# A hybrid RWKV-7 and band-attention block on one core: longer pauses between the steps of the recurrence's solve and chain, split head sums, and two tiles moved to other slots

## The chip, the core and the metric

The kernel runs on one core of a Trainium2 chip. The metric is the device time of one execution in microseconds. The time before is 867.89 us, the median of 3 runs (867.29 to 868.58). One execution was also recorded by the hardware profiler; all durations below are from it.

## What is computed

One residual block over 256 tokens of width 2048, in float32. The input is normalised and multiplied by one wide matrix, whose columns feed two branches; the branches are gated, projected, merged and sent through an output matrix. Cut to what matters:

```python
h = _rms_norm(x, pre_norm_g[l])
proj = h @ w_in[l]
p_r, p_k, p_v, z_r, q_a, k_a_att, v_a, z_a, m_r, m_a = jnp.split(proj, split_points, axis=-1)
y_r = _rwkv7_mixer(h, p_r, p_k, p_v, ...) * jax.nn.silu(z_r)
y_a = _chunk_band_attention(q_a, k_a_att, v_a, rel_bias[l]) * jax.nn.silu(z_a)
merged = (jax.nn.sigmoid(m_r + b_merge[l, 0]) * (y_r @ w_branch_rwkv[l])
          + jax.nn.sigmoid(m_a + b_merge[l, 1]) * (y_a @ w_branch_attn[l]))
x = x + _rms_norm(merged @ w_out[l], post_norm_g[l])
```

The RWKV-7 mixer is a recurrence over tokens for each of 16 heads of 64 channels, with a 64 by 64 state per head:

```python
sa = jnp.einsum('bhvk,bhk->bhv', state, -kkt)
state = (state * wt[:, :, None, :] + sa[..., None] * (kkt * at)[:, :, None, :]
         + vt[..., :, None] * kt[..., None, :])
yt = jnp.einsum('bhvk,bhk->bhv', state, rt)
```

## The kernel before

**The large products.** The weights arrive in chunks of 512 KB on SP's queue (three raw buffers, `NR`). ACT rounds a chunk to its high part (`wh_...`, line 92), DVE subtracts to get the low part (`wl_...`, line 93); there are four buffers of each (`NH`, `NL`), so that the low part of a chunk waits for the products of the chunk four before it. PE multiplies each high part with both halves of the activation (128x512) and each low part with the high half (128x256, lines 346 and 348). A product of 256 columns is four chunks long: `r`, `k` and `v` for the recurrence, `zr` and `za` for the gates, `q` and `ak` for attention. `va` and the later ones are 512 columns wide, and eight chunks long. A number behind a name is its first head pair: q2 covers the tiles 2 and 3; a digit behind that is the chunk (`wl_ak23` is the last chunk of ak2).

**Accumulators.** The large products share two accumulators in PSUM (`pm`, tag "mm", `acc_...`). `take` (lines 387 to 393) empties one: ACT copies one half, then DVE adds the other. The product after the next starts when that is done. All small products share four smaller ones (`ps`).

**The recurrence** is done in chunks of 64 tokens, for two groups of 8 heads (4 tiles, or two "duos" of two tiles). `group_decay` and `duo_front` (one for the duos 0, 2, 4, 6) build each duo's factors: head sums by a product with ones (`pn`, `pb`, through `head_sums`), decays (`pc`), the rate (`pa`), a long run on DVE, then the products of v (`pv`) and the chunk matrices A (`pA`). `group_back` then does for the whole group: the inverse of 16 by 16 blocks on DVE (`pr` and `S`, lines 599 and 601), from and to DRAM (`nb`, `N`, `rb`, `RA`, issued on ACT's queue); the solve (`T`, `z` line 620, `xx` line 628, `T2`, `z2` line 637, `x2` line 646, the transposes `pt` line 657 and their copies `BT`); and the chain over the four chunks c: `pw` (lines 667 and 671), its copy W on ACT (673), `pu` (677), its copies UV on DVE and ACT (679, 680), `pg` (691) and `py` (686, 694), and the new state SB on DVE (702, 704). pg and pw of the next chunk wait for UV and SB. In the trace a group's digit is left out of names; in the order it stands first (pg10 is group 1, chunk 0).

**What sets the order.** `run_plan` issues the large products chunk by chunk and prepares chunks two ahead. After each chunk `pump` takes steps of the small work, which is written as Python generators: up to `quota` steps of the queue `side` (the fronts), then `BQ` = 2 steps of the queue `back` (group_back, gates, attention). A step goes from one `yield` to the next. The plan after the projections of the recurrence is `q0 r2 v0 z0 v1 r6 r0 z2 q2 q4 q6 z4 r4 z6`, where q stands for q and ak, r for zr, z for za and v for va. A scheduler with a timeline of its own then orders each engine's instructions by the program's order and its own estimate, so that a step can move by some products.

**Slots that tie things.** The tile for q4 and later, `late`, takes the slot "A" (line 932) of group 1's A, and is free only when the chain of group 1 is done. The gate of za2 lies in a slot of tag "BT" (line 922), and its take waits for pg10 in both kernels; until then acc_za2 holds one of the two accumulators.

Of the kernel before, what the change touches and what calls it, by code (L numbers as in the profile page):

```python
# [9 lines left out]
F32 = mybir.dt.float32  # L10
# [9 lines left out]
QF = 2  # L20
QB = 2
BQ = 2
# [15 lines left out]
P = 128  # L38
D = 2048
DB = 1024  # L40
# [21 lines left out]
def kernel(ctx: ExitStack, tc, x, xt, vecs, w_in, wa1, w2, a2, w0, rel, w_br, w_ba, w_out, post_g, bm, out):  # L62
# [5 lines left out]
    bg = ctx.enter_context(tc.tile_pool(name="bg", bufs=1))  # L68
    tp = ctx.enter_context(tc.tile_pool(name="tp", bufs=2))
# [4 lines left out]
    def small(name):  # L74
        return ps.tile([P, 512], F32, tag="sm", name=name)
# [15 lines left out]
    def split(h, l, src, go=False):  # L91
        queue(ACT.activation(h, src, AF.Copy), go)  # L92
        queue(DVE.tensor_tensor(l, src, h.bitcast(F32), op=ALU.subtract), go)  # L93
# [143 lines left out]
    def step(d, n):  # L237
        while n > 0 and d:
            try:
                next(d[0])  # L240
                n -= 1
            except StopIteration:
                d.popleft()

# [198 lines left out]
    G = [None, None]  # L443
# [15 lines left out]

    def group_decay(g):  # L460
        d = G[g]
        for i in range(2):
            p = small(f"lw{g}{i}")
            PE.matmul(p, zw[0:65, i * P:(i + 1) * P], w2e[0:65, g * 512:(g + 1) * 512], start=True, stop=True)
            ACT.activation(d["s"][:, i, :], p, AF.Tanh, scale=0.5)
            DVE.tensor_scalar(d["s"][:, i, :], d["s"][:, i, :], 0.5, 0.5, op0=ALU.mult, op1=ALU.add)
            yield

    def head_sums(sq, nm):

        hi, lo = (tp.tile([P, 2, T], F32R, tag="ta", name=f"{nm}{n}") for n in "hl")
        split(hi, lo, sq)
        p = small(nm)
        for n, t in enumerate((hi, lo)):
            PE.matmul(p, onesr, t.rearrange("p m t -> p (m t)"), start=n == 0, stop=n == 1)
        return p

    def duo_front(j0):
# [19 lines left out]
        sq = tp.tile([P, 2, T], F32, tag="kk", name=f"sq{j0}")  # L498
        for m in range(2):
            ACT.activation(sq[:, m, :], k[:, m, :], AF.Square, scale=col(vt, V_KK + j0 + m))  # L500
        pn = head_sums(sq, f"pn{j0}")
        rn = tp.tile([P, 2, T], F32, tag="rn", name=f"rn{j0}", bufs=1)
        ACT.activation(rn.rearrange("p m t -> p (m t)"), pn, AF.Sqrt)
        yield
# [41 lines left out]
        yield  # L546
        for m in range(2):
            DVE.scalar_tensor_tensor(r[:, m, :], r[:, m, :], col(vt, V_RK + j0 + m), k[:, m, :], op0=ALU.mult, op1=ALU.mult)
        pb = head_sums(r, f"pb{j0}")
        DVE.tensor_tensor(d["bon"][:, qs, :], pb.rearrange("p (m t) -> p m t", m=2), v[:, qs, :], op=ALU.mult)  # L550
        yield
        for m in range(2):
            jj = q0 + m

            pv = small(f"pv{j0}{m}")
            for c in range(4):
                for h in range(2):
                    PE.matmul(pv[HS[1 - h], c * C:(c + 1) * C], v[:, jj, c * C:(c + 1) * C], cen[:, HS[h]], start=True, stop=True)
            ACT.activation(UV[64:128, 0, jj].rearrange("p c v -> p (c v)"), pv[64:128, 0:256], AF.Copy)
            ACT.activation(UV[0:64, 1, jj].rearrange("p c v -> p (c v)"), pv[0:64, 0:256], AF.Copy)  # L560
            yield
            pA = [small(f"pA{j0}{m}{h}") for h in range(2)]
            for c in range(4):
                for h in range(2):
                    PE.matmul(pA[h][:, c * P:(c + 1) * P], AB[HS[h], m, c, 2:4, :].rearrange("p a t -> p (a t)"),
                              AB[HS[h], m, c, 0:2, :].rearrange("p a t -> p (a t)"), start=True, stop=True)
            for h in range(2):
                DVE.tensor_tensor(A[:, h, jj], pA[h].rearrange("p (c a t) -> p c a t", c=4, a=2),
                                  msk.unsqueeze(1).to_broadcast([P, 4, 2, C]), op=ALU.mult)
            yield  # L570
# [5 lines left out]
    def group_back(g):  # L576
# [37 lines left out]
        for q in range(2):  # L614
# [3 lines left out]
            for u in range(8):  # L618
                for h in range(2):
                    PE.matmul(p1[q][HS[h], u * C:(u + 1) * C], Au[HS[h], h, q * 8 + u, 0, :], Tj[HS[h], u, :], start=True, stop=True)  # L620
        yield
        for q in range(2):
            Zt[q] = tp.tile([P, 8, C], F32, tag="W", name=f"Z{g}{q}", bufs=2)
            DVE.tensor_tensor(Zt[q], p1[q].rearrange("p (u t) -> p u t", u=8), m16.unsqueeze(1).to_broadcast([P, 8, C]), op=ALU.mult)
# [1 line left out]
            for u in range(8):  # L626
                for h in range(2):
                    PE.matmul(p2[q][HS[h], u * C:(u + 1) * C], Zt[q][HS[h], u, :], Rq[q][HS[h], u, :], start=True, stop=True)
        yield
        for q in range(2):  # L630
            DVE.tensor_tensor(Rq[q], p2[q].rearrange("p (u t) -> p u t", u=8), Rq[q], op=ALU.add)
            T2 = tp.tile([P, 8, 32], F32, tag="Z2", name=f"T2{g}{q}", bufs=3)
# [2 lines left out]
            for u in range(8):  # L635
                for h in range(2):
                    PE.matmul(p3[q][B2[h], u * 32:(u + 1) * 32], Au[A2[h], h, q * 8 + u, 0, 32:64], T2[A2[h], u, :], start=True, stop=True)
        yield
        for q in range(2):
            Z2 = tp.tile([P, 8, 32], F32, tag="Z2", name=f"Z2{g}{q}", bufs=3)  # L640
            ACT.activation(Z2[32:64].rearrange("p u t -> p (u t)"), p3[q][32:64, 0:256], AF.Copy)
# [2 lines left out]
            for u in range(8):  # L644
                for h in range(2):
                    PE.matmul(p4[q][A2[h], u * 32:(u + 1) * 32], Z2[B2[h], u, :], Rq[q][B2[h], u, 32:64], start=True, stop=True)
        yield
        for q in range(2):
            ACT.activation(Rq[q][0:32, :, 32:64], p4[q][0:32, 0:256].rearrange("p (u t) -> p u t", u=8), AF.Copy)
            DVE.tensor_copy(Rq[q][64:96, :, 32:64], p4[q][64:96, 0:256].rearrange("p (u t) -> p u t", u=8))  # L650
        yield
        BTs = []
        for c in range(3):
            BTs.append(tp.tile([P, 4, P], F32, tag="BT", name=f"BT{g}{c}", bufs=3))
# [1 line left out]
            for jj in range(4):  # L656
                PE.transpose(pt[:, jj * P:(jj + 1) * P], AB[jj // 2][:, jj % 2, c, 2:4, :].rearrange("p a t -> p (a t)"), ident)
            ACT.activation(BTs[c].rearrange("p j t -> p (j t)"), pt, AF.Copy)
        yield
        Y = bg.tile([P, 4, 4, C], F32, tag=("Y", "v")[g], name=f"Y{g}")  # L660
        d["Y"] = Y
        for c in range(4):
            pw = small(f"pw{g}{c}")
            for jj in range(4):
                for h in range(2):

                    PE.matmul(pw[HS[h], jj * C:(jj + 1) * C], A[:, h, jj, c, 0, :], UV[:, h, jj, c, :], start=jj == 0, stop=jj == 3 and not c)
            for jj in range(4):
                for h in range(2):
                    if c:  # L670
                        PE.matmul(pw[HS[h], jj * C:(jj + 1) * C], AB[jj // 2][:, jj % 2, c, 0, :], SB[:, jj, h, :], start=False, stop=jj == 3)
            W = tp.tile([P, 4, C], F32, tag="W", name=f"W{g}{c}", bufs=2)
            ACT.activation(W.rearrange("p j t -> p (j t)"), pw[:, 0:256], AF.Copy)
            pu = small(f"pu{g}{c}")
            for jj in range(4):
                for h in range(2):
                    PE.matmul(pu[HS[h], jj * C:(jj + 1) * C], R[HS[h], jj * 4 + c, :], W[HS[h], jj, :], start=True, stop=True)
            puv = pu[:, 0:256].rearrange("p (j t) -> p j t", j=4)
            DVE.tensor_copy(UV[HS[0], 0, :, c], puv[HS[0]])
            ACT.activation(UV[HS[1], 1, :, c], puv[HS[1]], AF.Copy)  # L680
            yield
            py = small(f"py{g}{c}")
            for jj in range(4):
                for h in range(2):
                    if c:
                        PE.matmul(py[HS[h], jj * C:(jj + 1) * C], SB[:, jj, h, :], AB[jj // 2][:, jj % 2, c, 1, :], start=jj == 0, stop=False)
            if c < 3:
                pg = small(f"pg{g}{c}")
                for jj in range(4):
                    for h in range(2):  # L690
                        PE.matmul(pg[HS[h], jj * C:(jj + 1) * C], BTs[c][:, jj, HS[h]], UV[:, h, jj, c, :], start=True, stop=True)
            for jj in range(4):
                for h in range(2):
                    PE.matmul(py[HS[h], jj * C:(jj + 1) * C], UV[:, h, jj, c, :], A[:, h, jj, c, 1, :], start=jj == 0 and not c, stop=jj == 3)
            if c < 3:
                pgv = pg[:, 0:256].rearrange("p (j t) -> p j t", j=4)
                for h in range(2):
                    fb = d["f"][HS[h], :, c].unsqueeze(2).to_broadcast([C, 4, C])
                    src = pgv[HS[h]]
                    sh = SB[HS[h], :, h, :]  # L700
                    if c:
                        DVE.tensor_tensor(sh, src, sh, op=ALU.add)
                        src = sh
                    DVE.tensor_tensor(sh, src, fb, op=ALU.mult)
            ACT.activation(Y[:, :, c, :], py[:, 0:256].rearrange("p (j t) -> p j t", j=4), AF.Copy)
            yield

        Yf = Y.rearrange("p j c t -> p j (c t)")
        for q in range(2):
# [111 lines left out]
    va = []  # L821

    def project_va(n):
        def done(acc):
            ACT.activation(va[0][:, n * 512:(n + 1) * 512], acc[:, 0, :], AF.Copy)
            DVE.tensor_copy(va[1][:, n * 512:(n + 1) * 512], acc[:, 1, :])
        def first_va():
            t = bg.tile([P, 2, DB], F32, tag="AB0", name="va")
            va.extend((t[:, 0, :], t[:, 1, :]))
        product(f"va{n}", wide_chunks(w_in, O_VA + n * 512, f"va{n}"), h_norm, True, done, quota=QB, before=None if n else first_va, wide=True)  # L830

# [132 lines left out]
    for c in range(4):  # L964
        ts = {}

        def load_bias(w, c=c, ts=ts):
            def f():
                if not (c or w):
                    start_merge()  # L970
                bb = tp.tile([P, 512], F32, tag="bb", name=f"bb{w}{c}")
                ts["b"] = bb
                tc.keep_in_program_order(nc.sync.dma_start(bb, bm[w * D + c * 512:w * D + (c + 1) * 512].partition_broadcast(P)))
                if not w:
# [121 lines left out]
```

## Time and profile before

| | |
|---|---|
| median of 3 runs | 867.89 us |
| profiled execution | 869.06 us |
| its span, first to last instruction | 867.1 us |
| PE busy | 846.8 us |
| DVE busy | 571.9 us |
| ACT busy | 425.0 us |
| mean granted clock of PE | 0.99 |

The span is 2.0 us less than the profiled execution's own time, for what lies around the instructions. "PEclk" or the clock in a row is the share of full speed that was granted to PE in that stretch. A row of the timeline gives the start, the busy time of the group, the engine, the line, out<-in with shapes and the count, and in brackets the idle time before it and what ended that. Lengths of neighbouring rows on one engine overlap a little, since instructions are pipelined; the distance from start to start is the time that counts.

### The profile page before, as it was taken

To read this page: it belongs to the slowest core of one execution; us is meant where nothing else is said; L and a number is where in the kernel's file an instruction comes from. 1 tells how busy PE (TensorE), PEld (TensorE's weight loads), DVE (VectorE), ACT (ScalarE), POOL (GpSimd) and SP (SyncE) were. 2 spreads that over 40 slices of the span, in tenths; PEclk is the share of its full clock that TensorE was granted. 3 is DMA by queue.
4 is the path that set the end of the run, shared out by engine and by line. 5 is a ranking of instruction groups with operands and counts; after the bars stand their busy time and mean duration, and the time that the engine had idled before them with its cause. 6 is when DMAs were issued, how large, how long until landed. Compare 5 with 4: busy or idle time off the path is not lost.

```text
span 867.1 us, 14007 instructions
## 1 busy us (share of the span) xinstructions
PE 846.8 (98%) x5624; PEld 718.0 (83%) x5624; DVE 571.9 (66%) x802; ACT 425.0 (49%) x601; POOL 17.7 (2%) x68
## 2 busy tenths in 40 slices
PE   8999999999899999999899999999999999999996
PEld 8998888887778888888787777888888888888896
DVE  7998896867539968644597865555555565555555
ACT  7558564535345444443466664444444444444442
POOL 2010000000010000000000000000000000000000
PEclk9999999999899999999999999999999999999999
DMA  9826544663143557544265445676576577676562
GB/s 299 226 85 195 171 150 126 200 178 102 50 133 113 175 154 215 161 127 142 74 194 173 145 141 174 194 206 196 189 206 199 194 216 241 209 254 199 194 192 98
DMA packets 119427, 149.35 MB, mean 172 GB/s; under 512 B 13633, under 2 KB 82241, under 8 KB 118978
## 3 DMA queue, kind: packets, MB, share of 16 engines
q1 hardware_dynamic: 106258, 140.53, 52.8%
q10 hardware_dynamic: 13104, 7.93, 3.1%
q8 instruction: 44, 0.72, 0.3%
q14 instruction: 21, 0.17, 0.1%
HBM read 145.82 MB, written 2.62 MB: 171 GB/s over the span
## 4 chain that ended last, share of the span: by engine, by line
PE 95%; DVE 2%; ACT 1%; DMA 1%; issue 1%; ACTq 0%; DVEq 0%
PE acc_mr L284 10%; PE acc_ma L284 10%; PE acc_o L284 10%; PE acc_va L284 5%; PE acc_ur L284 5%; PE acc_ua L284 5%; PE acc_q L348 4%; PE acc_zr L348 4%; PE acc_za L348 4%; PE acc_ak L348 3%; PE acc_k L284 3%; PE acc_r L348 3%; PE acc_v L348 3%; PE acc_zr L346 2%; PE acc_za L346 2%; PE acc_k L348 2%
## 5 line engine op out<-in xcount | busy, mean ns | idle before, releaser
L284 PE MATMUL acc_mr<-wh_mr,hn 128*128 128x512 f32 x256 | 82.1, 395 | 0.0
L284 PE MATMUL acc_ma<-wh_ma,hn 128*128 128x512 f32 x256 | 79.5, 390 | 0.0
L93 DVE TENSOR_TENSOR wl_ma<-raw_ma,wh_ma 128x1024 fp32r<-128x1024 f32 x32 | 39.2, 1225 | 42.2 <-ACT wh_ma L92 42.2
L93 DVE TENSOR_TENSOR wl_o<-raw_o,wh_o 128x1024 fp32r<-128x1024 f32 x31 | 37.9, 1225 | 33.0 <-ACT wh_o L92 32.9
L93 DVE TENSOR_TENSOR wl_mr<-raw_mr,wh_mr 128x1024 fp32r<-128x1024 f32 x32 | 39.2, 1224 | 28.8 <-ACT wh_mr L92 28.8
L284 PEld LDWEIGHTS acc_mr<-wh_mr,hn 128*128 128x128 f32 x256 | 47.9, 188 | 10.7 <-issue 1.2
L92 ACT ACTIVATE wh_ma<-raw_ma 128x1024 fp32r<-128x1024 f32 x32 | 34.0, 1061 | 46.3 <-PE acc_ma L284 21.4
L284 PEld LDWEIGHTS acc_ma<-wh_ma,hn 128*128 128x128 f32 x256 | 48.1, 188 | 9.9
L92 ACT ACTIVATE wh_mr<-raw_mr 128x1024 fp32r<-128x1024 f32 x32 | 33.9, 1060 | 43.4 <-PE acc_ua L284 19.9
L92 ACT ACTIVATE wh_o<-raw_o 128x1024 fp32r<-128x1024 f32 x31 | 32.9, 1060 | 39.1 <-PE acc_o L284 26.4
L284 PE MATMUL acc_mr<-wl_mr,hn 128*128 128x512 f32 x128 | 50.2, 392 | 0.0
L284 PE MATMUL acc_o<-wh_o,mgh 128*128 128x512 f32 (+1 forms) x140 | 49.9, 357 | 0.0
L284 PE MATMUL acc_o<-wl_o,mgh 128*128 128x512 f32 (+1 forms) x140 | 49.9, 356 | 0.0
L284 PE MATMUL acc_ma<-wl_ma,hn 128*128 128x512 f32 x128 | 49.9, 389 | 0.0
L284 PE MATMUL acc_va<-wh_va,hn 128*128 128x512 f32 x128 | 41.2, 397 | 0.0
L348 PE MATMUL acc_q<-hn,wh_q 128*128 128x512 f32 x128 | 35.5, 415 | 2.2 <-DVE late L393 1.7
L348 PE MATMUL acc_zr<-hn,wh_zr 128*128 128x512 f32 x128 | 35.0, 412 | 0.3 <-DVE aq L393 0.3
L348 PE MATMUL acc_za<-hn,wh_za 128*128 128x512 f32 x128 | 34.5, 401 | 0.0
L348 PE MATMUL acc_ak<-hn,wh_ak 128*128 128x512 f32 x128 | 34.2, 400 | 0.1
L93 DVE TENSOR_TENSOR wl_va<-raw_va,wh_va 128x1024 fp32r<-128x1024 f32 x16 | 19.5, 1221 | 22.0 <-ACT wh_va L92 14.7
L93 DVE TENSOR_TENSOR wl_ua<-raw_ua,wh_ua 128x1024 fp32r<-128x1024 f32 x16 | 19.6, 1224 | 20.4 <-ACT wh_ua L92 20.4
L93 DVE TENSOR_TENSOR wl_ur<-raw_ur,wh_ur 128x1024 fp32r<-128x1024 f32 x16 | 19.6, 1224 | 17.9 <-ACT wh_ur L92 17.9
(481 smaller groups left out, 2102.7 us busy)
## 6 DMA issues: line engine op xcount, KB each, us to landing
raw_mr<-w_in_d SPq DMA_DIRECT2D x32, 512.0 KB, 3.7
raw_ma<-w_in_d SPq DMA_DIRECT2D x32, 512.0 KB, 3.7
raw_o<-w_out_d SPq DMA_DIRECT2D x32, 512.0 KB, 4.5
raw_v<-w_in_d SPq DMA_DIRECT2D x16, 512.0 KB, 3.8
raw_q<-w_in_d SPq DMA_DIRECT2D x16, 512.0 KB, 3.6
raw_ak<-w_in_d SPq DMA_DIRECT2D x16, 512.0 KB, 3.7
raw_zr<-w_in_d SPq DMA_DIRECT2D x16, 512.0 KB, 4.4
raw_va<-w_in_d SPq DMA_DIRECT2D x16, 512.0 KB, 3.7
```

Source lines behind the costliest of these rows:

```text
L92: queue(ACT.activation(h, src, AF.Copy), go)
L93: queue(DVE.tensor_tensor(l, src, h.bitcast(F32), op=ALU.subtract), go)
L284: PE.matmul(d, u, v, start=first and n == 0, stop=last and n == len(ops) - 1)
L346: PE.matmul(acc[:, m, 0:256], wl[:, k, ms], a[:, 0, :], start=False, stop=g == ng - 1 and k == 3)
L348: PE.matmul(acc[:, m, :], wh[:, k, ms], a.rearrange("p n t -> p (n t)"), start=g == 0 and k == 0, stop=False)
```

## The change

1. `step` subtracts what a generator yields, so that a step can count for more than one.
2. In the solve and the chain of `group_back` each `yield` becomes `yield BQ`: one step fills the whole pause after a chunk. There is one more such pause between W and pu.
3. `group_decay` of group 0 pauses once for a whole `QF` at its start.
4. `head_sums` is cut in two: `head_parts` rounds and splits the operand, then comes a pause, then the products.
5. `duo_front` of group 1 does not go on to `pv` and `pA` until the chain of group 0 is done ("solved").
6. The tile `va` gets a slot of its own instead of "AB0"; the merge's bias tiles use the slots "xs".

```diff
@@ step
-                next(d[0])
-                n -= 1
+                n -= next(d[0]) or 1
@@ group_decay
+        if not g:
+
+            yield QF
@@ head_sums
-    def head_sums(sq, nm):
-
+    def head_parts(sq, nm):
         hi, lo = (tp.tile([P, 2, T], F32R, tag="ta", name=f"{nm}{n}") for n in "hl")
         split(hi, lo, sq)
+        return hi, lo
+
+    def head_sums(parts, nm):
+
         p = small(nm)
-        for n, t in enumerate((hi, lo)):
+        for n, t in enumerate(parts):
@@ duo_front
-        pn = head_sums(sq, f"pn{j0}")
+        parts = head_parts(sq, f"pn{j0}")
+        yield
+        pn = head_sums(parts, f"pn{j0}")
...
-        pb = head_sums(r, f"pb{j0}")
+        parts = head_parts(r, f"pb{j0}")
+        yield
+        pb = head_sums(parts, f"pb{j0}")
         DVE.tensor_tensor(d["bon"][:, qs, :], pb.rearrange("p (m t) -> p m t", m=2), v[:, qs, :], op=ALU.mult)
         yield
+
+        while g and "solved" not in G[0]:
+            yield
@@ group_back: after z, xx, z2, x2, the copies of x2, pt, UV and Y
-        yield
+        yield BQ
@@ group_back, chain
             ACT.activation(W.rearrange("p j t -> p (j t)"), pw[:, 0:256], AF.Copy)
+            yield BQ
             pu = small(f"pu{g}{c}")
...
+        d["solved"] = True
@@ first_va
-            t = bg.tile([P, 2, DB], F32, tag="AB0", name="va")
+            t = bg.tile([P, 2, DB], F32, tag="va", name="va")
@@ load_bias
-                bb = tp.tile([P, 512], F32, tag="bb", name=f"bb{w}{c}")
+                bb = tp.tile([P, 512], F32, tag="xs", name=f"bb{w}{c}", bufs=2)
```

The number of instructions on each engine stays the same. SP's and POOL's orders stay the same; PE's order changes from the middle of acc_ak0 to the start of acc_q6.

On PE, at the change from acc_ak0 to acc_zr2, this stood before:

```order
L686 MATMUL py01_2064<-AB00_473,SB_162 64x64 x4
L686 MATMUL py01_2064<-AB01_474,SB_162 64x64 x4
L691 MATMUL pg01_2073<-UV0_856,BT01_1916 64x64
L694 MATMUL py01_2064<-A0_855,UV0_856 64x64
L667 MATMUL pw02_2095<-UV0_856,A0_855 64x64 x8
L691 MATMUL pg01_2073<-UV0_856,BT01_1916 64x64 x7
L694 MATMUL py01_2064<-A0_855,UV0_856 64x64 x7
L671 MATMUL pw02_2095<-SB_162,AB00_473 64x64 x4
L671 MATMUL pw02_2095<-SB_162,AB01_474 64x64 x4
L348 MATMUL acc_zr2_2848<-hn_660,wh_zr20_2745 128x512 x8
L346 MATMUL acc_zr2_2848<-hn_660,wl_zr20_2746 128x256 x8
```

and this stands there now:

```order
L679 MATMUL pw00_2057<-UV0_886,A0_885 64x64 x8
L345 MATMUL acc_ak0_2550<-hn_660,wl_ak03_2584 128x256 x3
L480 MATMUL pb4_2096<-pb4h_2092,onesr_112 128x512
L690 MATMUL pu00_2100<-W00_2066,RA_882 64x64 x8
L480 MATMUL pb4_2096<-pb4l_2093,onesr_112 128x512
L347 MATMUL acc_zr2_2725<-hn_660,wh_zr20_2631 128x512 x8
L345 MATMUL acc_zr2_2725<-hn_660,wl_zr20_2632 128x256 x8
L347 MATMUL acc_zr2_2725<-hn_660,wh_zr21_2679 128x512 x4
L704 MATMUL pg00_2134<-UV0_886,BT00_1995 64x64 x8
L707 MATMUL py00_2133<-A0_885,UV0_886 64x64 x8
L679 MATMUL pw01_2176<-UV0_886,A0_885 64x64 x8
L347 MATMUL acc_zr2_2725<-hn_660,wh_zr21_2679 128x512 x4
```

The chain's chunk 1 moved from before acc_zr2 into it, and pb4, which stood behind acc_zr2, now stands before it.

On PE, between acc_q2 and acc_ak2 (the second product of q's kind and the one after it), this stood before:

```order
L348 MATMUL acc_q2_4170<-hn_660,wh_q23_4187 128x512 x5
L346 MATMUL acc_q2_4170<-hn_660,wl_q23_4188 128x256 x8
L646 MATMUL x210_3079<-RA_852,Z210_3076 32x32
L646 MATMUL x211_3099<-RA_852,Z211_3096 32x32
L646 MATMUL x210_3079<-RA_852,Z210_3076 32x32 x15
L646 MATMUL x211_3099<-RA_852,Z211_3096 32x32 x15
L657 MATMUL pt10_3153<-ident_101,AB10_1235 128x128 x2
L657 MATMUL pt10_3153<-ident_101,AB11_1236 128x128 x2
L657 MATMUL pt11_3160<-ident_101,AB10_1235 128x128 x2
L657 MATMUL pt11_3160<-ident_101,AB11_1236 128x128 x2
L348 MATMUL acc_ak2_4262<-hn_660,wh_ak20_4209 128x512 x8
```

and this stands now, from acc_q2's last product to acc_q4's first:

```order
L345 MATMUL acc_q2_4152<-hn_660,wl_q23_4188 128x256 x8
L347 MATMUL acc_ak2_4262<-hn_660,wh_ak20_4209 128x512 x8
L345 MATMUL acc_ak2_4262<-hn_660,wl_ak20_4210 128x256 x8
L347 MATMUL acc_ak2_4262<-hn_660,wh_ak21_4231 128x512 x8
L345 MATMUL acc_ak2_4262<-hn_660,wl_ak21_4232 128x256 x8
L347 MATMUL acc_ak2_4262<-hn_660,wh_ak22_4256 128x512 x8
L345 MATMUL acc_ak2_4262<-hn_660,wl_ak22_4257 128x256 x8
L347 MATMUL acc_ak2_4262<-hn_660,wh_ak23_4279 128x512 x8
L345 MATMUL acc_ak2_4262<-hn_660,wl_ak23_4280 128x256 x8
L632 MATMUL z10_3084<-T10_3082,A1_1798 64x64 x16
L632 MATMUL z11_3103<-T11_3101,A1_1798 64x64 x16
L347 MATMUL acc_q4_4354<-hn_660,wh_q40_4301 128x512 x8
```

Group 1's solve, from z10 to pt, moved from acc_q2 to behind acc_ak2 and into acc_q4.

On DVE, around the take of aq2 (which empties acc_q2), this stood before:

```order
L93 TENSOR_TENSOR wl_ak23_4280<-raw_ak23_4281,wh_ak23_4279 128x1024
L393 TENSOR_TENSOR aq2_4253<-acc_q2_4170,aq2_4253 128x512
L650 COPY RA_852<-x210_3079 32x8x32
L650 COPY RA_852<-x211_3099 32x8x32
L93 TENSOR_TENSOR wl_q40_4302<-raw_q40_4303,wh_q40_4301 128x1024
L93 TENSOR_TENSOR wl_q41_4324<-raw_q41_4325,wh_q41_4323 128x1024
L679 COPY UV1_1883<-pu10_3185 64x4x64
```

and this stands now, from the operation behind wl_ak23 to the take of ak2:

```order
L611 TENSOR_TENSOR pr1_3003<-S1_3002,N1_3000 128x196
L392 TENSOR_TENSOR aq2_4253<-acc_q2_4152,aq2_4253 128x512
L613 TENSOR_REDUCE S1_3002<-pr1_3003 128x14
L611 TENSOR_TENSOR pr1_3003<-S1_3002,N1_3000 128x225
L613 TENSOR_REDUCE S1_3002<-pr1_3003 128x15
L93 TENSOR_TENSOR wl_q40_4302<-raw_q40_4303,wh_q40_4301 128x1024
L628 STREAM_TRANSPOSE T10_3082<-RA_882 128x512
L628 STREAM_TRANSPOSE T11_3101<-RA_882 128x512
L93 TENSOR_TENSOR wl_q41_4324<-raw_q41_4325,wh_q41_4323 128x1024
L93 TENSOR_TENSOR wl_q42_4349<-raw_q42_4350,wh_q42_4348 128x1024
L93 TENSOR_TENSOR wl_q43_4388<-raw_q43_4389,wh_q43_4387 128x1024
L392 TENSOR_TENSOR ak2_4345<-acc_ak2_4262,ak2_4345 128x512
```

The last steps of group 1's inverse (pr and S of 14 and 15) moved from before acc_q2's end to behind the take of aq2, and the transposes T10 and T11 with them.

More of the change, by code (lines that the diff above doesn't have):

```diff
@@ L628, in group_back @@
                     PE.matmul(p2[q][HS[h], u * C:(u + 1) * C], Zt[q][HS[h], u, :], Rq[q][HS[h], u, :], start=True, stop=True)
-        yield
+        yield BQ
         for q in range(2):
@@ L637, in group_back @@
                     PE.matmul(p3[q][B2[h], u * 32:(u + 1) * 32], Au[A2[h], h, q * 8 + u, 0, 32:64], T2[A2[h], u, :], start=True, stop=True)
-        yield
+        yield BQ
         for q in range(2):
@@ L646, in group_back @@
                     PE.matmul(p4[q][A2[h], u * 32:(u + 1) * 32], Z2[B2[h], u, :], Rq[q][B2[h], u, 32:64], start=True, stop=True)
-        yield
+        yield BQ
         for q in range(2):
@@ L650, in group_back @@
             DVE.tensor_copy(Rq[q][64:96, :, 32:64], p4[q][64:96, 0:256].rearrange("p (u t) -> p u t", u=8))
-        yield
+        yield BQ
         BTs = []
@@ L658, in group_back @@
             ACT.activation(BTs[c].rearrange("p j t -> p (j t)"), pt, AF.Copy)
-        yield
+        yield BQ
         Y = bg.tile([P, 4, 4, C], F32, tag=("Y", "v")[g], name=f"Y{g}")
@@ L673, in group_back @@
             ACT.activation(W.rearrange("p j t -> p (j t)"), pw[:, 0:256], AF.Copy)
+            yield BQ
             pu = small(f"pu{g}{c}")
@@ L680, in group_back @@
             ACT.activation(UV[HS[1], 1, :, c], puv[HS[1]], AF.Copy)
-            yield
+            yield BQ
             py = small(f"py{g}{c}")
@@ L705, in group_back @@
             ACT.activation(Y[:, :, c, :], py[:, 0:256].rearrange("p (j t) -> p j t", j=4), AF.Copy)
-            yield
+            yield BQ
+        d["solved"] = True
         Yf = Y.rearrange("p j c t -> p j (c t)")
```

## The prediction

> **What bounds the kernel now.** I read the page first, then the waits of PE, then PE's busy time by stretches of 20 us, then the timelines of PE and DVE where a stretch is not full. The page gives the span, PE's share and the chain that ended last:
>
> ```profile
> span 867.1 us, 14007 instructions
> PE 846.8 (98%) x5624; PEld 718.0 (83%) x5624; DVE 571.9 (66%) x802; ACT 425.0 (49%) x601; POOL 17.7 (2%) x68
> PE 95%; DVE 2%; ACT 1%; DMA 1%; issue 1%; ACTq 0%; DVEq 0%
> ```
>
> PE is the path. The change leaves the number of matmuls as it is, so it can move the time only through PE's idle time and PE's clock. PE's waits (time, times, longest) name where it is late inside the two groups of the recurrence:
>
> ```profile
> PE pw L671 <- DVE SB L704: 2.4, 1, 2.4
> PE xx L628 <- issue: 1.7, 2, 1.1
> PE acc_q L348 <- DVE late L393: 1.7, 1, 1.7
> PE pu L677 <- ACT W L673: 1.6, 3, 0.7
> ...
> PE pg L691 <- DVE UV L679: 0.8, 1, 0.8
> ```
>
> The stretches (length, then busy time of PE, PEld, DVE, ACT, POOL, then the granted clock) place them:
>
> ```profile
> 180.00:200.00 20.00, 18.89 (x268) 16.33 (x267) 13.40 (x19) 8.16 (x11) 0.00 (x0) 1.00 0.53 146
> 200.00:220.00 20.00, 17.03 (x295) 14.45 (x293) 16.39 (x29) 11.61 (x22) 0.00 (x0) 1.00 0.27 80
> 220.00:240.00 20.00, 17.89 (x166) 14.74 (x168) 9.74 (x16) 6.24 (x10) 0.00 (x0) 0.83 0.18 53
> ...
> 340.00:360.00 20.00, 19.34 (x212) 16.84 (x211) 12.06 (x16) 6.23 (x7) 0.31 (x1) 1.00 0.69 197
> ...
> 380.00:400.00 20.00, 19.49 (x224) 16.72 (x223) 10.48 (x16) 8.55 (x12) 0.00 (x0) 1.00 0.42 132
> 400.00:420.00 20.00, 17.78 (x222) 14.74 (x220) 8.91 (x13) 7.76 (x13) 0.00 (x0) 1.00 0.43 133
> 420.00:440.00 20.00, 19.97 (x100) 16.18 (x101) 14.83 (x22) 8.17 (x10) 0.00 (x0) 0.91 0.18 53
> ```
>
> PE lacks 1.11 + 2.97 + 2.11 = 6.2 us in group 0's solve and chain (180 to 240) and 0.66 + 0.51 + 2.22 + 0.03 = 3.4 in group 1's (340 to 440). A lowered clock comes on top. Two pairs of narrower stretches show it:
>
> ```profile
> 219.30:223.50 4.20, 1.44 (x16) 1.12 (x16) 4.03 (x10) 2.19 (x5) 0.00 (x0) 0.83 0.00 0
> 223.50:241.40 17.90, 17.85 (x161) 14.96 (x162) 6.40 (x9) 5.44 (x8) 0.00 (x0) 0.85 0.26 71
> 417.00:421.00 4.00, 2.23 (x31) 1.78 (x27) 1.49 (x3) 2.77 (x6) 0.00 (x0) 0.88 0.43 131
> 421.00:433.00 12.00, 12.00 (x59) 9.21 (x58) 7.26 (x5) 4.78 (x5) 0.00 (x0) 0.90 0.16 45
> ```
>
> After the 2.4 us wait the drop costs 0.17 x 4.2 + 0.15 x 17.9 = 3.4 us; after the 1.7 us wait it costs 0.12 x 4 + 0.10 x 12 = 1.7. So 6.2 + 3.4 + 3.4 + 1.7 = 14.7 us of the profiled execution stand in the stretch that the change touches. That is the most it can win.
>
> **Part one: group 0 gains.** Before, the chain's steps for chunks 0 to 2 stood back to back on PE ahead of acc_zr2. Now each of the steps after the first has four or more large products ahead of it (over 0.9 us), mostly far more, so the waits of pw, pu and pg there are covered. In return acc_zr2's first products now stand behind pb4, the second head sum of duo 4, on both halves. Rows of PE and of DVE that price this:
>
> ```profile
> 184.91 2.08 PE L620 MATMUL z<-T,A 64*64 64x64 f32 x64
> ...
> 209.13 0.38 PE L346 MATMUL acc_ak<-hn,wl_ak 128*128 128x256 f32 x1
> ...
> 210.82 0.71 PE L512 MATMUL pc<-cum,s 128*128 128x130 f32 x4
> ```
>
> ```profile
> 201.81 0.93 DVE L650 COPY RA<-x 32x256 f32<-32x256 f32 x2 [1.24 <-ACT RA L649]
> ...
> 212.00 0.20 DVE L526 RECIPROCAL fr<-pp 128x8 f32<-128x8 f32 x1 [0.55 <-ACT pp L515]
> ...
> 213.36 0.87 DVE L704 TENSOR_TENSOR SB<-pg,f 64x256 f32<-64x256 f32 x2
> ...
> 217.03 0.42 DVE L679 COPY UV<-pu 64x256 f32<-64x256 f32 x1
> ...
> 219.48 0.88 DVE L548 SCALAR_TENSOR_TENSOR r<-r,vt,k 128x256 f32<-128x256 f32 x2
> ...
> 222.08 0.69 DVE L93 TENSOR_TENSOR pb4l<-r,pb4h 128x512 fp32r<-128x512 f32 x1
> 222.80 0.69 DVE L393 TENSOR_TENSOR aq<-acc_q,aq 128x512 f32<-128x512 f32 x1
> ```
>
> PE did from z (184.91) to the end of acc_ak0 (209.3) what it will do again, and the pc and pa of duo 4's second tile move into this stretch (about 0.8), so PE comes to pb4 at 210.1. DVE's run from fr to the end of r took 212.00 to 220.36, 8.4 us, with 0.87 + 0.42 of the chain in it, which go; the copies of x2 (0.93) and one wl (about 1.15) come into it: 9.2. Its start, pc41, now stands among acc_ak0's third chunk, at about 201.5 by the lengths of the products ahead of it; with the 1.2 us from pc (210.82) to fr, r is done at 201.5 + 1.2 + 9.2 = 211.9. Behind r come a wl (1.15), pb4l (0.6 in step) and the take of aq0 (0.6): acc_zr2 starts at 214.2 or so. PE has 1.3 us of products in between, so it waits 214.2 - 210.1 - 1.3 = 2.8; I take 3.0 in several pieces, between 0 (the pumps fit) and 5.1 (all that the rows show less xx). The wait of xx, 1.1, keeps its place. Group 0 after: 4.1 us of idle time against 6.2, and the clock's 3.4 may go: its cause, the 2.4 us wait among small products, is gone, and of the new pieces none has to be longer than 1.7.
>
> **Part two: group 1 loses.** duo_front(6) now waits for "solved", so A of group 1 is finished inside zr0 and no longer in va1, and the Neumann steps on DVE end behind acc_q2. Rows of PE and of DVE around this place before:
>
> ```profile
> 352.00 2.08 PE L620 MATMUL z<-T,A 64*64 64x64 f32 x64
> ...
> 364.93 1.12 PE L346 MATMUL acc_q<-hn,wl_q 128*128 128x256 f32 x8
> ...
> 368.27 2.12 PE L348 MATMUL acc_ak<-hn,wh_ak 128*128 128x512 f32 x8
> ...
> 434.96 2.00 PE L348 MATMUL acc_q<-hn,wh_q 128*128 128x512 f32 x8
> ...
> 437.75 2.00 PE L348 MATMUL acc_ak<-hn,wh_ak 128*128 128x512 f32 x8
> ```
>
> ```profile
> 338.94 0.56 DVE L599 TENSOR_TENSOR pr<-S,N 128x225 f32<-128x225 f32 x1
> ...
> 340.00 0.38 DVE L601 TENSOR_REDUCE S<-pr 128x15 f32<-128x225 f32 x1
> ...
> 350.57 1.30 DVE L616 STREAM_TRANSPOSE T<-RA 128x512 f32<-128x512 f32 x2 [6.58 <-DMA RA<-rb]
> ...
> 366.27 1.22 DVE L93 TENSOR_TENSOR wl_ak<-raw_ak,wh_ak 128x1024 fp32r<-128x1024 f32 x1 [1.64 <-ACT wh_ak L92]
> 367.52 0.69 DVE L393 TENSOR_TENSOR aq<-acc_q,aq 128x512 f32<-128x512 f32 x1
> ```
>
> Three waits follow one from another. First, acc_ak2 needs the accumulator of acc_q2 (the other one is held by acc_za2, whose take waits for group 1's pg10 in both kernels). From acc_q2's last product (366.05) to acc_ak2 there were 2.2 us, wl_ak23 and the take, which x2 and pt filled; now nothing stands there, and one pr more does on DVE: 2.2 to 2.8, I take 2.5. Second, z10 stands behind all four chunks of acc_ak2, 4 x 2.79 (434.96 to 437.75 is one chunk) = 11.2 us. But S is done only 1.3 us behind the take of aq2 (a reduce, 0.56, 0.38), and from S to z it took 340.38 to 352.00, 11.6 us, through two DMAs and the transposes: 12.9 - 11.2 = 1.7. Third, acc_q4 needs the take of ak2, which stands on DVE behind T10, T11 and three wl of q4: 3 x 1.14 + 0.69 = 4.1 us from z10's start, of which z covers 2.0: 2.1. In all 2.5 + 1.7 + 2.1 = 6.3; from 2.2 (only the first is sure) to 9. The transfers that carry S to RA are issued on ACT's queue and move with it; behind them stand wh_q41 to wh_q43 there, whose wl stand behind T10 and T11 on DVE, and these wait for the same transfers, so that this queueing is in the 2.1. SP's and POOL's queues keep their order.
>
> Then the rest of the solve and the chain's first step stand in one block ahead of acc_ak4, which waits for the take of za2: W 0.7, UV 0.8 by the waits quoted, and about 0.5 for SB: 2.0. The last steps stand in one block ahead of acc_q6: W 0.5, UV 0.8, SB 1.2 (between 0.5 and the 2.4 of its row), and the 1.7 for the late tile as before: 4.2. Both blocks from 2.2 (what they cost now) to 9. The xx wait goes, as more than a chunk of acc_q4 covers it. Group 1 after: 6.3 + 2.0 + 4.2 = 12.5 against 3.4.
>
> The clock: with 4 us idle out of 6 around z10 and the late block longer than before, I count 1.7 at acc_q4 and 1.7 at acc_q6, by the cheaper of the two rows; from 0 to three times 3.4.
>
> **The rest costs nothing.** The head sums' pieces hold the same instructions. Group 0's extra pause at the start moves its two tanh pieces among stretches where PE is full at this place in order and time. The tag of va and the tag of the bias tiles change no engine's order outside this stretch; if either made a load wait, PE's 20.00 of 20 in the later stretches would show it.
>
> **The sum.** After: 4.1 + 12.5 idle and 3.4 of clock = 20.0; before 14.7: slower by 5.3. The profiled execution took 869.06, so 874.4; on the median of 867.89 this is 873.2.
>
> **Rivals.** (1) Group 1's waits don't come: the products on PE run late enough, or DVE early enough, that S, the takes and the chain find cover as they do now. Group 1 stays at 3.4 + 1.7 and group 0 gains 2.1 + 3.4: 5.5 faster, 862.4. For it: DVE is busy 9 to 12 us of 20 in this stretch, and the transfers had slack in the old order. Against it: each of the three waits is a dependence on one accumulator with no product left between. It decides where group 1's waits and clock stay under 10.6 us instead of 15.9. (2) Both sides cancel: only the first of the three waits comes and the clock drops once: 20.0 - 3.8 - 1.7 = 14.5, no change, 867.7. (3) No gap is long enough to lower the clock: 16.6 against 14.7, 1.9 slower, 869.8. [...] Against it: the waits of 2.4 and of 1.7 lowered it already. [...] (4) The clock drops at all three places, by 3.4 each: 16.6 + 10.2 - 14.7 = 12.1 slower, 880.0.
>
> **How the numbers follow.** A difference of 0.2%, 1.7 us, is about what a measurement of this kernel can tell from none. Forecast 0.50 (its own range 870 to 878); rival 1, 0.20; rival 2, 0.11; rival 3, 0.13; rival 4, 0.06. Rival 3 lies just above the 0.2% bound, and I count a tenth or so of it as no change. Faster 0.20, same 0.12, slower 0.68. The range goes from 864, in the middle between rivals 1 and 2, to 878.5, near rival 4: it leaves out most of rival 1 and rival 4.
>
> **What would show it.** Right: in the stretch of acc_zr2 PE no longer waits for SB, and waits of about 3 us in all for pb4 and aq; acc_ak2 waits some 2.5 for the take of aq2, z10 for T, acc_q4 some 2 for the take of ak2; two blocks of small products ahead of acc_ak4 and acc_q6 hold 4 us or more of waits. Wrong: acc_ak2 or z10 without a wait, or a full clock from acc_q4 on.

## The result, and the profile after

The changed kernel took 873.54 us, the median of 4 runs (872.36 to 874.94), beside 868.09 for the kernel before (4 runs). The ratio is 1.0064, with a 95% interval of 1.0046 to 1.0082: slower by 5.5 us. The profiled execution took 874.06 us with a span of 872.2.

PE's waits in the changed kernel, in the form of those shown of before (total, times, longest):

```profile
PE acc_ak L347 <- DVE aq L392: 4.0, 1, 4.0
PE pb L480 <- ACT pb4h L92: 2.4, 1, 2.4
PE acc_q L347 <- DVE late L392: 1.7, 1, 1.7
PE acc_q L347 <- DVE ak L392: 1.3, 1, 1.3
```

The waits of group 0's chain (SB 2.4, most of W and UV) are gone. Two new ones stand on top, at the accumulator of acc_q2 and at pb4. The same stretches as before:

```profile
180.00:200.00 20.00, 20.00 (x275) 17.35 (x274) 17.54 (x25) 12.25 (x17) 0.00 (x0) 1.00 0.44 129
200.00:220.00 20.00, 17.58 (x189) 14.54 (x188) 14.18 (x25) 8.66 (x16) 0.00 (x0) 0.83 0.29 90
220.00:240.00 20.00, 20.00 (x214) 16.44 (x211) 8.80 (x13) 7.70 (x11) 0.00 (x0) 1.00 0.39 113
...
340.00:360.00 20.00, 16.00 (x91) 13.99 (x90) 17.55 (x41) 7.49 (x8) 0.30 (x1) 0.94 0.71 222
360.00:380.00 20.00, 18.73 (x148) 16.25 (x147) 8.46 (x11) 5.78 (x6) 0.00 (x0) 0.89 0.47 134
380.00:400.00 20.00, 18.78 (x349) 16.12 (x348) 10.41 (x17) 8.60 (x16) 0.00 (x0) 1.00 0.34 109
400.00:420.00 20.00, 18.33 (x242) 15.34 (x242) 9.48 (x15) 6.14 (x9) 0.00 (x0) 1.00 0.34 106
420.00:440.00 20.00, 17.70 (x134) 14.05 (x135) 10.88 (x14) 8.65 (x13) 0.00 (x0) 0.91 0.09 28
```

From 180 to 240 PE now lacks 2.4 us where it lacked 6.2; from 340 to 440 it lacks 10.5 where it lacked 3.4. Two landmarks divide the difference, since the same products lie ahead of each in both kernels: the start of acc_q2 and the start of acc_q6. Their rows before, and then after:

```profile
347.95 2.00 PE L348 MATMUL acc_q<-hn,wh_q 128*128 128x512 f32 x8
...
420.03 3.67 PE L348 MATMUL acc_q<-hn,wh_q 128*128 128x512 f32 x8 [1.69 <-DVE late L393]
```

```profile
343.77 2.00 PE L347 MATMUL acc_q<-hn,wh_q 128*128 128x512 f32 x8
...
359.10 3.78 PE L347 MATMUL acc_ak<-hn,wh_ak 128*128 128x512 f32 x8 [4.00 <-DVE aq L392]
...
364.34 1.99 PE L347 MATMUL acc_ak<-hn,wh_ak 128*128 128x512 f32 x8
...
372.79 2.08 PE L632 MATMUL z<-T,A 64*64 64x64 f32 x64
...
425.11 3.30 PE L347 MATMUL acc_q<-hn,wh_q 128*128 128x512 f32 x8 [1.69 <-DVE late L392]
```

Up to acc_q2 the change wins 347.95 - 343.77 = 4.2 us. From acc_q2 to acc_q6 it takes 81.3 us instead of 72.1 and loses 9.3. The sum, 5.1, is the whole difference of the two spans (872.2 - 867.1).

### The profile page after: what moved, and what is told of

It reads as the page before. It is cut to its first block, busy times and chain, and to the rows that moved or that the text cites. A ratio compares the mean times of both kernels' runs of the same rounds, so it can differ in the third digit from the quotient of the medians.

```text
span 872.2 us, 14011 instructions
## 1 busy us (share of the span) xinstructions
PE 847.6 (97%) x5624; PEld 717.9 (82%) x5624; DVE 571.5 (66%) x802; ACT 424.5 (49%) x601; POOL 17.5 (2%) x68
## 4 chain that ended last, share of the span: by engine, by line
PE 94%; DVE 3%; ACT 1%; DMA 1%; issue 0%; ACTq 0%; DVEq 0%
PE acc_mr L283 10%; PE acc_ma L283 10%; PE acc_o L283 9%; PE acc_va L283 5%; PE acc_ua L283 5%; PE acc_ur L283 5%; PE acc_q L347 4%; PE acc_zr L347 4%; PE acc_za L347 3%; PE acc_ak L347 3%; PE acc_r L347 3%; PE acc_v L347 3%; PE acc_k L283 2%; PE acc_za L345 2%; PE acc_zr L345 2%; PE acc_k L347 2%
## 5 line engine op out<-in xcount | busy, mean ns | idle before, releaser
L92 ACT ACTIVATE wh_ak<-raw_ak 128x1024 fp32r<-128x1024 f32 x16 | 16.8, 1058 | 32.2 <-PE acc_q L347 15.6
```

## The experiments

**The theory.** Group 1 loses because its A comes late: the inverse on DVE is then still running when acc_q2 ends, and the take of aq2 stands in the middle of it. It comes late because the front of duo 6 stands in line behind that of duo 4, which waits for group 0's chain. **The rival:** group 1's own steps of solve and chain, which now take whole pauses, cost the time.

Each run is compared with the kernel before on the same chip (867.87 us in the first four, 866.87 in the last four); the ratio is the one on record and can differ by up to 0.2% from the quotient of the two medians. "The stretch" is the time from acc_q2 to acc_q6, 72.1 us before and 81.3 after.

**1. rotate.** While duo 4's front waits, duo 6's goes ahead to the same place.

```diff
-                n -= next(d[0]) or 1
+                y = next(d[0]) or 1
+                if y == "wait":
+                    d.rotate(-1)
+                    y = 1
+                n -= y
...
         while g and "solved" not in G[0]:
-            yield
+            yield "wait"
...
-        if q0:
+        d["fronts"] = d.get("fronts", 0) + 1
+        if d["fronts"] == 2:
             back.append(group_back(g))
```

> The changed kernel, with one thing added: while the front of duo 4 waits for the chain of group 0, the front of duo 6 goes ahead of it and waits at the same place itself. In the order group 1's A is then finished some 27 us of PE work earlier, and z of group 1 stands inside acc_q2 again, as before the change. Theory (lateness: group 1 loses because its A comes late, and it comes late because the front of duo 6 stands in line behind that of duo 4, which waits for the longer chain of group 0): acc_ak2 waits under 1.5 us, the stretch from acc_q2 to acc_q6 goes from 81.3 back to 72 to 74 us, group 0 keeps its gain of 4.2, time 863 to 867. Rival (group 1 loses because its own steps of solve and chain take whole pauses): the stretch stays at 79 or more, time 871 to 874.

Measured: 863.86 us, ratio to before 0.9948 (0.9933 to 0.9962). The stretch, by the rows of acc_q2 and acc_q6 on PE, with that of acc_ak2 between them:

```profile
343.63 2.00 PE L351 MATMUL acc_q<-hn,wh_q 128*128 128x512 f32 x8
...
365.00 2.14 PE L351 MATMUL acc_ak<-hn,wh_ak 128*128 128x512 f32 x8 [0.33 <-DVE aq L396]
...
416.77 2.11 PE L351 MATMUL acc_q<-hn,wh_q 128*128 128x512 f32 x8 [1.69 <-DVE late L396]
```

It is 73.1 us long, the wait of acc_ak2 is 0.33, and group 0 keeps its 4.3. The pauses of group 1 are all still there. The lateness was the cause, and the rival falls.

**2. rotate_za.** As rotate; the gate of za2 also moves.

```diff
-                z = tp.tile([P, 2, T], F32, tag="BT" if j0 else "zs", name=f"za{j0}", bufs=3 if j0 else 1)
+                z = bg.tile([P, 2, T], F32, tag="AB0", name=f"za{j0}") if j0 else tp.tile([P, 2, T], F32, tag="zs", name=f"za{j0}", bufs=1)
```

> As rotate, and the gate of za2 lies in the slot AB0, which the change made free, so that its take no longer waits for pg10 of group 1 and acc_za2 gives its accumulator back at once. Theory (lateness): the waits for the takes of aq2 and ak2 are gone altogether, acc_q4 and acc_ak4 start without a wait; 0 to 2 us under rotate, 862 to 866. Rival (own pauses): 871 to 874, as nothing in the pauses changes.

Measured: 864.51 us, ratio 0.9970 (0.9954 to 0.9987): no difference from rotate that the two intervals can tell, and the gain of 0 to 2 us on it isn't shown. The profiled execution is one of the longest of its twelve (867.70 at a mean clock of 0.987; the six at 0.995 or more took 862.0 to 863.7), so its rows don't stand for the median. In it the waits for aq2 and ak2 are gone, as expected, but the stretch is 73.3 us, no shorter than rotate's. The time comes back ahead of acc_q6, in the stretch that ends the chain of group 1:

```profile
400.00:420.00 20.00, 16.69 (x200) 14.18 (x197) 7.39 (x11) 7.12 (x13) 0.00 (x0) 0.83 0.35 106
```

PE lacks 3.3 us there and the clock 17%. In rotate the same 20 us lack 2.3, at full clock. Products that could have covered the chain's last steps had run earlier; that this is the whole reason isn't shown.

**3. no_pause.** All `yield BQ` of `group_back` made `yield`, and the one between W and pu taken out.

```diff
-        yield BQ
+        yield
...
             ACT.activation(W.rearrange("p j t -> p (j t)"), pw[:, 0:256], AF.Copy)
-            yield BQ
```

> The changed kernel, with every whole pause in the solve and chain of both groups made a plain yield again, and without the extra one between W and pu; the wait for the chain, the split head sums and the slots stay. Theory (lateness): group 1's A is still later than before the change, acc_ak2 still waits 2 to 4 us, and in group 0 some of the old waits for SB and UV come back: 870 to 874. Rival (own pauses): the stretch from acc_q2 to acc_q6 goes back to 72 to 74 us, time 865 to 868.

Measured: 874.85 us, ratio 1.0077 (1.0062 to 1.0092), slower than either expected. Group 0's waits are back: acc_q2 starts only 0.8 earlier than before.

```profile
347.11 2.00 PE L347 MATMUL acc_q<-hn,wh_q 128*128 128x512 f32 x8
```

So without the pauses 3.3 of group 0's 4.2 us go. The stretch is 81.3, as long as with the pauses, which speaks against the rival once more. The wait of acc_ak2 is even 5.6:

```profile
PE acc_ak L347 <- DVE aq L392: 5.6, 1, 5.6
PE pg L703 <- DVE UV L691: 2.9, 2, 2.3
PE pw L683 <- DVE SB L716: 2.6, 3, 1.5
```

Here the inverse was over when acc_q2 ended, and the take of aq2 was late on ACT, not on DVE: it stood behind the eight transfers from rb to RA on ACT's queue.

```profile
358.39 4.25 ACTq L620 DMA_DIRECT2D RA<-rb  x8
362.69 0.60 ACT L391 ACTIVATE aq<-acc_q 128x512 f32<-128x512 f32 x1 [5.21 <-DMA RA<-rb]
```

The order says one thing more. If the wait for "solved" is also taken out of this kernel, no row of the order changes on PE, DVE or ACT; nor does any if that wait alone is put into the kernel before. The split of the head sums, put into the kernel before by itself, gives the order of no_pause on every engine. So its pauses alone make group 1's A late.

**4. no_split.** The pauses between `head_parts` and the products of pn and pb taken out.

```diff
         parts = head_parts(sq, f"pn{j0}")
-        yield
...
         parts = head_parts(r, f"pb{j0}")
-        yield
```

> The changed kernel with the pauses inside the head sums taken out again. In the order group 1's A is done some 3 us of PE work earlier and z of group 1 stands in acc_ak2's last chunk. Theory (lateness): the wait of acc_ak2 falls from 4.0 by 1 to 3 us, group 0 is as it was: 870 to 873. Rival (the split itself costs, by the pauses that it adds to the fronts): under 870.

Measured: 874.57 us, ratio 1.0075 (1.0058 to 1.0092): outside what either expected. acc_ak2 waits 4.0 as before the edit, though A is done 16.1 us ahead of acc_q2 where it was 12.8. Most of that lead passes before N is back from DRAM: the inverse starts 5.7 us ahead of acc_q2 where it was 4.8. The wait for pb4h, which the split was thought to leave alone, grew to 5.5:

```profile
PE pb L480 <- ACT pb4h L92: 5.5, 1, 5.5
PE acc_ak L347 <- DVE aq L392: 4.0, 1, 4.0
```

With it, acc_q2 starts at 347.02:

```profile
347.02 2.00 PE L347 MATMUL acc_q<-hn,wh_q 128*128 128x512 f32 x8
```

Without the split, too, group 0 keeps only 0.9 of its 4.2 us. It takes both sets of pauses for the gain of group 0, and one set suffices for the loss of group 1. Either alone, in the fronts (no_pause) or in the solve and chain (no_split), makes group 1 lose 9 to 10 us: its stretch is 81.3 and 81.9. They don't add.

**5. after_za_slot.** The changed kernel with the edit of rotate_za alone.

> The changed kernel with the gate of za2 in the free slot AB0, and nothing else: acc_za2 gives its accumulator back at once, so that acc_ak2 no longer waits for the take of aq2. A of group 1 stays as late as in the changed kernel. Theory (what the lateness costs is paid at the accumulators): the 4.0 us of acc_ak2 and the 1.3 of acc_q4 go, and with them the clock's drop there; the late block ahead of acc_q6 gets longer, as the chain has less room: 866 to 870. Rival (late steps cost the same wherever they stand): 872 to 874.

Measured: 868.11 us, ratio 1.0017 (1.0004 to 1.0030). A comes as late as in the changed kernel, 12.8 us ahead of acc_q2, yet the stretch is 74.6 us. acc_ak2 starts without a wait, right at the end of acc_q2:

```profile
345.09 2.00 PE L347 MATMUL acc_q<-hn,wh_q 128*128 128x512 f32 x8
...
356.26 2.00 PE L347 MATMUL acc_ak<-hn,wh_ak 128*128 128x512 f32 x8
...
419.69 2.54 PE L347 MATMUL acc_q<-hn,wh_q 128*128 128x512 f32 x6 [1.69 <-DVE late L392]
```

So lateness costs through the accumulators: with za2 holding one, PE has nothing else to run while DVE ends the inverse. With both free the late chain costs its own waits only; they pile up in one block ahead of acc_q6 (PE lacks 5.6 of the 20 us from 400 to 420). Of the 9.3 us that group 1 lost, 6.7 are back and 2.5 stay.

**6. own_pauses_out.** Group 1's solve and chain step as before the change.

```diff
-        yield BQ
+        yield None if g else BQ
...
-            yield BQ
+            if not g:
+                yield BQ
```

> The changed kernel with the whole pauses left in group 0 alone; group 1's solve and chain step as before the change. On PE the order comes out the same as the changed kernel's. Theory (lateness): 872.5 to 874.5, no difference. Rival (own pauses of group 1): 864 to 868.

Measured: 875.34 us, ratio 1.0082 (1.0057 to 1.0108). No better than the changed kernel; the rival's 864 to 868 is out, and the theory's 872.5 to 874.5 is missed by 0.8. On ACT and on DVE, too, the order is the changed kernel's but for one pair of neighbours each: group 1's own pauses hardly move a row, so they can't be what costs the 9.3 us. The other side of this is that the run is almost the changed kernel once more, and shows how far its time can spread. Its four runs spread from 871.02 to 876.90 with mean granted clocks from 0.994 to 0.984.

**7. after_aq_slot.** aq0 and ak0 get slots of their own; va goes back to AB0.

```diff
-            t = bg.tile([P, 2, DB], F32, tag="va", name="va")
+            t = bg.tile([P, 2, DB], F32, tag="AB0", name="va")
...
-                    t = tp.tile([P, 2, T], F32, tag=tag, name=f"a{what}{j0}")
+                    t = tp.tile([P, 2, T], F32, tag=tag if j0 else f"a{what}", bufs=2 if j0 else 1, name=f"a{what}{j0}")
```

> The changed kernel with slots of their own for aq0 and ak0, so that the take of aq0 doesn't wait for the last use of k4 by the front of duo 4 (va goes back to AB0 for room). In the order acc_zr2 then stands ahead of pb4, and the wait for pb4h with 2.4 us and the lowered clock after it should go: acc_zr2 starts at about 209 where it was 213.7. Theory (the clock drops because of that wait): up to 2.4 + 3.4 = 5.8 faster up to acc_za2, and A of group 1 stays late: 867 to 871 in all. Rival (the clock drops there by the small products alone): 2 us faster at most, 871 to 873.

Measured: 871.41 us, ratio 1.0045 (1.0028 to 1.0062). The time lies just above the theory's 867 to 871 and within the rival's 871 to 873, so it doesn't decide between them; the clock does. Around acc_zr2 the edit did what was expected, and acc_zr2 starts at 209.47. One stretch of the changed kernel, and the same of this one:

```profile
208.80:218.30 9.50, 7.08 (x36) 5.56 (x36) 5.21 (x9) 3.05 (x5) 0.00 (x0) 0.64 0.37 112
```

```profile
208.80:218.30 9.50, 9.50 (x77) 8.00 (x76) 8.51 (x12) 4.08 (x7) 0.00 (x0) 1.00 0.52 149
```

The wait of 2.4 us is gone and with it the lowered clock, 0.36 x 9.5 = 3.4 us. Of these 3.4 some 0.3 had cost nothing, as they fell into the wait itself, so that 5.5 us could be won and not 5.8. By acc_q2 (340.33) 3.4 of them are left; about 1.7 went back to idle time at xx and at the chain's end (19.08 and 19.19 busy of 20 in two stretches that were full), and some 0.4 aren't traced. Group 1 stays late, and its stretch is 82.7.

**8. rotate_aq.** Edits 1 and 7 together.

> The front of duo 6 goes ahead as in the run rotate, and aq0 and ak0 have slots of their own as in the run after_aq_slot. Theory: both gains add, 863.9 - 5.8 = 858, within 857 to 861. Rival (the clock drops by the small products alone): 861 to 864.

Measured: 862.63 us, ratio 0.9948 (0.9931 to 0.9965). That number lies in the rival's band, but not for the rival's reason: wait and lowered clock are gone here too (9.50 of 9.50 at clock 1.00 from 208.8 to 218.3). Yet acc_za2 starts at 331.00, only 1.45 earlier than in rotate (332.45), where 5.8 were hoped for. Some 1.4 us went to the last py and the variance products, which now wait for ACT, and 0.5 to xx. Another 1.1 were lost ahead of all that the edits touch: the same rows of acc_q stand at 186.38 in rotate and at 187.47 here; what cost them isn't shown. The rest, some 1.3 us, isn't traced and stays open. Against rotate there is no gain that the two ratios can tell; both beat the kernel before by 0.5%, and the changed one by 1.1%.

## Why the prediction was right, point by point

**The sign and the size** came out: 873.2 was forecast, 873.54 measured, slower by 5.3 and 5.5. Both terms were too large, by 1.3 and by 1.5 us, and that these errors cancelled is luck: group 0 was to win 2.1 + 3.4 = 5.5 and won 4.2; group 1 was to lose 9.1 + 1.7 = 10.8 and lost 9.3.

**Group 0.** The forecast put acc_zr2 at 214.2; it started at 213.69. The rows of PE around it:

```profile
208.28 0.62 PE L345 MATMUL acc_ak<-hn,wl_ak 128*128 128x256 f32 x3
211.32 0.79 PE L480 MATMUL pb<-pb4h,onesr 128*128 128x512 f32 x1 [2.42 <-ACT pb4h L92]
212.04 1.12 PE L690 MATMUL pu<-W,RA 64*64 64x64 f32 x16
213.09 0.79 PE L480 MATMUL pb<-pb4l,onesr 128*128 128x512 f32 x1
213.69 3.61 PE L347 MATMUL acc_zr<-hn,wh_zr 128*128 128x512 f32 x8
```

The step that failed is that the 3.0 us would come "in several pieces" of at most 1.7, and that the clock's 3.4 would go. The wait came in one piece of 2.42 and took the clock along, just as the old one had: 0.50 from 210.66 to 217.49, which costs 3.1 us behind the wait. The idle time was smaller than forecast, 2.4 from 180 to 240 and not 4.1, which hid part of this miss. The 1.1 of xx, which was to keep its place, went in this execution; other kernels of this document with the same order there show 0.3 to 1.2. So up to that much of group 0's 4.2 us is this execution's and not the change's.

**Group 1, the three waits.** Forecast 2.5, 1.7 and 2.1; measured 4.0, 0 and 1.3. DVE's rows of the changed kernel show why the first was larger:

```profile
354.23 1.22 DVE L93 TENSOR_TENSOR wl_ak<-raw_ak,wh_ak 128x1024 fp32r<-128x1024 f32 x1
...
356.84 1.22 DVE L93 TENSOR_TENSOR wl_ak<-raw_ak,wh_ak 128x1024 fp32r<-128x1024 f32 x1
357.97 0.47 DVE L611 TENSOR_TENSOR pr<-S,N 128x196 f32<-128x196 f32 x1
358.36 0.68 DVE L392 TENSOR_TENSOR aq<-acc_q,aq 128x512 f32<-128x512 f32 x1
...
359.93 0.39 DVE L613 TENSOR_REDUCE S<-pr 128x15 f32<-128x225 f32 x1
...
370.80 1.31 DVE L628 STREAM_TRANSPOSE T<-RA 128x512 f32<-128x512 f32 x2 [4.98 <-DMA RA<-rb]
```

I had counted only one wl and one pr between acc_q2's end (355.1) and the take; DVE had fallen behind: it was in the middle of one wl, with another and five steps of the inverse still to do. The second wait didn't come, which by the prediction's own sign ("z10 without a wait") counts against it. The distance was right, though: T began at 370.80, and four chunks of 2.79 from 359.10 would have ended at 370.3, before z10 could start. But the first of them ran at a lowered clock and took 5.2 us (359.10 to 364.34), and these 2.5 us more covered the wait. So the lowered clock there cost less in the end than it took. The sum of the three waits, 5.3, was near the 6.3; none of its pieces was.

**The blocks.** Forecast 2.0 and 4.2. The late one shows 0.59 + 0.95 + 0.53 + 1.69 = 3.8, in order UV, SB, W and the late tile:

```profile
416.73 0.33 PE L704 MATMUL pg<-UV,BT 128*64 128x64 f32 x2 [0.59 <-DVE UV L692]
...
419.47 1.13 PE L683 MATMUL pw<-SB,AB 128*64 128x64 f32 x16 [0.95 <-DVE SB L717]
421.13 0.68 PE L690 MATMUL pu<-W,RA 64*64 64x64 f32 x16 [0.53 <-ACT W L685]
```

The early one shows 0.5 + 0.5, and its SB wait didn't come.

**The clock.** 1.7 was forecast at acc_q4 and 1.7 at acc_q6. It fell at acc_ak2 instead, during the longer wait, and stayed low for longer:

```profile
354.90:359.10 4.20, 0.20 (x3) 0.00 (x1) 4.10 (x9) 0.84 (x2) 0.00 (x0) 0.80 0.58 188
359.10:366.00 6.90, 6.90 (x24) 5.84 (x25) 2.38 (x4) 1.06 (x1) 0.00 (x0) 0.63 0.40 105
...
425.20:431.20 6.00, 6.00 (x24) 5.09 (x25) 1.67 (x2) 2.99 (x4) 0.00 (x0) 0.72 0.00 0
```

The first row is time in which PE waited, so its lowered clock cost nothing. The second gives 0.37 x 6.9 = 2.6 us, and acc_q6 0.28 x 6 = 1.7 as forecast.

**The cause of the lateness** was named too narrowly. The prediction put it down to the wait for "solved". That wait alone moves nothing, as the order shows. The pauses in the head sums make duo 6's front late without it (no_pause). The pauses in group 0's solve and chain do so through it (no_split): they delay the end of that chain, for which duo 4's front waits, and duo 6's stands in line behind it. So the prediction had half of the cause. Letting duo 6's front go ahead to the wait (rotate) took the loss away.

**The cheap parts.** Without the pause at the start of `group_decay` the order of PE, DVE and ACT stays row for row the same; I didn't run it. The slots were not run by themselves either.

## What to carry to other kernels

A longer pause between dependent steps hides their latency (here the 2.4 us of the wait for SB), but it also pushes back all that is queued behind them; ask which later step has a deadline, here the take that frees an accumulator, and whether the pause moves work past it. Where two accumulators serve all large products, a tile whose slot comes free late can turn a delay on another engine into idle time of PE (4.0 us for one on DVE, 5.6 for one on ACT here): give the slot first. A wait that is removed in one place doesn't pay in full where the products that ran earlier leave the next block without cover, as ahead of acc_q6 in after_za_slot (5.6 us of idle time there).

## What the runs showed of the hardware

**The clock.** Between 20 and 850 us of the profiled executions of the kernel before and of the changed kernel, the granted clock was 1.00 but for five stretches at 0.50. In the kernel before they go from 222.08 to 228.90 and from 420.05 to 423.46, in the changed kernel from 210.66 to 217.49, from 357.43 to 364.25 and from 425.70 to 429.11. Each begins during a wait of PE or less than 0.6 us behind it; in this order the waits are 2.37 (for SB), 1.69 (for the late tile), 2.42 (for pb4h), 4.00 (for the take of aq2) and 1.69 us (for the late tile).

The length of a single wait does not tell whether a lowered clock follows. Ahead of acc_q6 the same wait of 1.69 us was followed by a lowered clock in the kernel before and in the changed kernel, and by a full clock in rotate. The 5 us from 1.77 before the start of acc_q6, first in the kernel before, at a clock of 0.68:

```profile
418.26:423.26 5.00, 3.31 (x10) 2.58 (x9) 1.29 (x2) 2.40 (x5) 0.00 (x0) 0.68 0.21 74
```

then in the changed kernel, at 0.74:

```profile
423.34:428.34 5.00, 3.31 (x11) 2.56 (x10) 1.29 (x2) 2.40 (x5) 0.00 (x0) 0.74 0.00 0
```

and in rotate, at 1.00 there and in the 6 us behind:

```profile
415.00:420.00 5.00, 3.31 (x20) 2.86 (x19) 1.29 (x2) 3.46 (x7) 0.00 (x0) 1.00 0.22 75
420.00:426.00 6.00, 6.00 (x35) 4.41 (x33) 5.08 (x4) 3.71 (x4) 0.00 (x0) 1.00 0.29 87
```

PE was busy for 3.31 of the 5 us in all three; what makes the difference isn't shown.

I estimate that the stretch from 425.70 to 429.11 at 0.50 cost 0.50 x 3.41 = 1.7 us, as PE was busy throughout it. That from 357.43 to 364.25 cost less than half of its length: PE waited for the first 1.67 us of it, until 359.10.
